# Compressed-key scores in a sparse-attention block: one matmul of 128 columns a head for two of 64, and a VectorE add for the second part

## The chip, the cores and the metric

The kernel runs on one core of a Trainium2 chip. The metric is the time of one execution in microseconds (us), the median of several runs; the profile comes from one further execution. In the profile, PE is TensorE's matrix multiply and PEld its load of weights, DVE is VectorE, ACT ScalarE, POOL GpSimd and SP SyncE.

## The reference

One decoder block on 1024 tokens of width 1024, in float32: a normalisation and an input projection, two branches side by side (sparse attention with 8 heads of 64 in 2 groups, and retention with 4 heads of 128), sigmoid gates that merge the branches, an output projection and a feed-forward network of width 2816. The sparse attention has three parts for each query: attention over compressed keys (one for each 16 tokens), over the 8 best blocks of 64 tokens, and over a window of 512. The change touches the first:

```python
kc = rms_norm(compress_blocks(k_cmp, cmp_pe[0], cmp_w1[0], cmp_w2[0]), k_g[0])
c_dist = (t_pos[:, None] - c_end[None, :]).astype(f32)
sc = jnp.einsum('btgrd,bngd->bgrtn', qg, kc).astype(f32) * scale - slopes[:, :, None, None] * c_dist
p_cmp = masked_softmax(sc, c_dist >= 0)
o_cmp = jnp.einsum('bgrtn,bngd->btgrd', p_cmp.astype(vc.dtype), vc)
...
imp = jnp.einsum('bgtn,nj->bgtj', p_cmp.sum(axis=2), overlap)
_, sel_idx = lax.top_k(imp, n_top)
```

So the weights over the compressed keys also choose which blocks the second part reads.

## The kernel before

Matmuls run on float32 values split in a high and a low part (`split`, L371: ScalarE copies the high part, VectorE subtracts it to get the low one), and a product is three matmuls, high by high, high by low and low by high. Every Python generator in the kernel (a stream) yields operations to a planner (`Sched`, L159). The planner keeps a clock of its own for each engine and a cost for each operation, and emits next the operation that it thinks can start first; equal ones go by priority. The instructions of an engine then stand in that order for good, with semaphores between the engines. Other costs in one place therefore change the order in many.

Attention works through 16 units `us` (2 groups of heads by 8 tiles of 128 queries). `cmp_all` (L1304) does the compressed part of a unit: the scores of the four heads of the group in one PSUM bank `s` (L1313 to L1315), then the scaled sum with the distance table Mc and the running minimum (`ttr`, L1299, a custom VectorE instruction that writes the probabilities' tile P and the minimum m; the profile has it as L1302 cP), the exponential on ScalarE, the reciprocal and the gate, and Pd, P doubled side by side and scaled, on POOL. Four transposes of Pd and a split make pcT, with which `consume_all` (L1440) starts the unit's output. From the fourth tile on `select` chooses the blocks and writes `comb`. `kc` holds the 64 compressed keys of a group twice: `kc[:, g, 0]` has high over low parts on its 128 partitions, `kc[:, g, 1]` the same with the parts exchanged; the stationary operand `qt[u][:, 0, r, :]` is the same for both, and L1314 and L1315 add the two products in PSUM.

`produce_all` (L1379) makes the scores of the window and of the chosen blocks (psS<-kT,qt, then L1302 P), and shares the two scores banks of `s_ring` (L1265) with `cmp_all`. `consume_all` transposes P (psT<-ident,P), splits it (pT) and multiplies with the values (psO<-pT,vv). `finish` sends a unit's output y to DRAM (`y_scr`).

What else is there runs between these as filler, with lower priority. `merge_gates` (L1270) makes the gates of the merge (psF or psS <-H,wh, then zs to `z_scr`). When the gates are done, `y_loads` brings the branches' outputs back from DRAM (yraw<-y_scr) and `y_split` writes them over H; `branch1` (L1559) multiplies the retention branch with its weights, sixteen outputs of twelve matmuls (psF<-H,wh), scales them with the gate (sg) and writes them to `u_scr`. `merge_main` (L1581) does the same for the attention branch: its first two outputs go to the banks of `f_ring` (psF), and behind them, in the order of the queue, the six banks S, S, S, O, T, T of `u_ring` (L1523) in turn, once the last unit's y is on its way (L1587). `mx_loads` (L1596) reads `u_scr` back into the mx tiles, which are allocated only when all of attention's memory is given back (L1626 to L1639), and `merge_out` (L1602) loads the gate (sgm<-z_scr), multiplies it with the output in PSUM, which frees the bank, and adds to mx. All these loads go through SyncE's one queue, in the planner's order. Behind the merge stand the output projection (psS<-wo,H) and the feed-forward network.

Of the kernel before, what the change touches and what calls it, by code (L numbers as in the profile page):

```python
# [9 lines left out]
F32 = mybir.dt.float32  # L10
# [3 lines left out]
ALU = mybir.AluOpType  # L14
# [26 lines left out]
def nel(ap):  # L41
    n = 1
    for d in ap.shape[1:]:
        n *= d
    return n
# [212 lines left out]
def kernel(  # L258
# [50 lines left out]
    def mm(o, l, r, start, stop):  # L309
        n = nel(r)  # L310
        c = max(108.0, n * RATE[0] + 3) if r.dtype == F32R else 4 * max(53.5, n * 0.4167 + 1)
        return Op("pe", c, 100, [o], [l, r],
                  lambda: pe.matmul(o, l, r, start=start, stop=stop, skip_group_check=True))  # L313

    def tr(o, i):
        if i.dtype == F32R:
            return Op("pe", 56, 100, [o], [i], lambda: pe.transpose(o.bitcast(F32R), i, identr))
        return Op("pe", 109, 100, [o], [i], lambda: pe.transpose(o, i, ident))  # L318

    def ac(o, i, scale=1.0, func=AF.Copy, bias=None, accum=None):  # L320
        kw, ins, outs, c = {}, [i], [o], (51 if i.tensor.name.startswith("ps") else 93) + 0.833 * nel(o)
        for a in (scale, bias, accum):
            if a is not None and not isinstance(a, float):
                c += 93
        if bias is not None:
            kw["bias"] = bias
            ins.append(bias)
        if accum is not None:
            kw["accum_out"] = accum
            outs.append(accum)  # L330
        if not isinstance(scale, float):
            ins.append(scale)
        return Op("act", c, 150, outs, ins, lambda: act.activation(o, i, func, scale=scale, **kw))  # L333

    def vop(o, ins, fn, eng=None, fast=False):
        n = nel(o)
        if eng is gp:
            return Op("gp", 70 + 2.4 * n, 150, [o], ins, fn)
        c = 61 if any(nel(i) == 1 < n for i in ins) else 0
        return Op("dve", 69 + c + (0.52 if fast else 1.04) * n, 130, [o], ins, fn)  # L340

    def tt(o, a, b, op, eng=None):
        return vop(o, [a, b], lambda: (eng or dve).tensor_tensor(o, a, b, op), eng)  # L343

    def ts(o, a, s1, s2=None, op0=ALU.mult, op1=None, eng=None, fast=True):
        ins = [a] + [s for s in (s1, s2) if s is not None and not isinstance(s, (int, float))]
        if op1 is None:
            return vop(o, ins, lambda: (eng or dve).tensor_scalar(o, a, s1, None, op0=op0), eng, fast)  # L348
        return vop(o, ins, lambda: (eng or dve).tensor_scalar(o, a, s1, s2, op0=op0, op1=op1), eng, fast)

    def stt(o, a, s, b, op0, op1, eng=None):
        ins = [a, b] + ([] if isinstance(s, float) else [s])
        return vop(o, ins, lambda: (eng or dve).scalar_tensor_tensor(o, a, s, b, op0=op0, op1=op1), eng)  # L353

    def recip(o, i):
        return vop(o, [i], lambda: dve.reciprocal(o, i))
# [118 lines left out]
    kc = att.tile([128, 2, 2, HD], F32R, name="kc")  # L475
# [4 lines left out]
    Mc = att.tile([128, 128], F32, name="Mc")[:, 0:120]  # L480
# [344 lines left out]
    qt, qref = {}, {}  # L825
# [12 lines left out]
    def q_drop(u):  # L838
        qref[u] -= 1
        if not qref[u]:  # L840
            rings["q"].release(qt[u])
# [392 lines left out]
    ap_ = es.enter_context(tc.tile_pool(name="ap", bufs=2))  # L1234
# [64 lines left out]
    def ttr(o, a, b, sc, init, acc):  # L1299
        ins = [a, b] + ([] if isinstance(init, float) else [init])  # L1300
        return Op("dve", (77 if isinstance(init, float) else 138) + 1.04 * nel(o), 130, [o, acc], ins,
                  lambda: dve.tensor_tensor_reduce(o, a, b, -sc, init, ALU.add, ALU.min, acc))  # L1302

    def cmp_all():  # L1304
        yield Wait(lambda: "ct" in fl)
        for u in us:
            g, i = u
            yield Wait(lambda: u in qt)
            P = ap_.tile([128, 4, 64], F32, name="cP", bufs=1)
            l = small.tile([128, 4], F32, name="cl")  # L1310
            m = small.tile([128, 4], F32, name="cm")
            s = yield Alloc(s_ring)
            for r in range(4):  # L1313
                yield mm(s[:, r * 64:(r + 1) * 64], qt[u][:, 0, r, :], kc[:, g, 0, :], True, False)  # L1314
                yield mm(s[:, r * 64:(r + 1) * 64], qt[u][:, 0, r, :], kc[:, g, 1, :], False, True)  # L1315
            q_drop(u)
            for r in range(4):
                yield ttr(P[:, r, :], s[:, r * 64:(r + 1) * 64], Mc[:, 56 - 8 * i:120 - 8 * i],
                          2.0 ** -(4 * g + r + 1), 3e38, m[:, r:r + 1])
            s_ring.release(s)  # L1320
            for r in range(4):
                yield ac(P[:, r, :], P[:, r, :], scale=-1.0, func=AF.Exp, bias=m[:, r:r + 1], accum=l[:, r:r + 1])
            rl = small.tile([128, 4], F32, name="crl")
            c = small.tile([128, 4], F32, name="cc")
            yield recip(rl, l)
            yield tt(c, rl, gate[:, i, 4 * g:4 * g + 4, 0], ALU.mult)
            if i == 0:
                yield ts(c, c, valid0)
            Pd = ap_.tile([128, 4, 2, 64], F32, name="cPd", bufs=1)
            yield tt(Pd, P[:, :, None, :].to_broadcast([128, 4, 2, 64]),  # L1330
                     c[:, :, None, None].to_broadcast([128, 4, 2, 64]), ALU.mult, gp)
            if i >= 4:
                pn = ap_.tile([128, 4, 64], F32, name="cpn", bufs=1)
                yield tt(pn, P, rl[:, :, None].to_broadcast([128, 4, 64]), ALU.mult)
                yield stt(pn, pn, TINY, pn, ALU.is_ge, ALU.mult)
                sch.spawn(select(u, pn), 2)
            pt = yield Alloc(pc_ring)
            p = yield Alloc(t_ring)
            for r in range(4):
                yield tr(p[:, r * 128:(r + 1) * 128], Pd[:, r].rearrange("p a n -> p (a n)"))  # L1340
            yield ac(pt, p)
            yield tt(pt[64:128, :], p[64:128, :], pt[64:128, :].bitcast(F32), ALU.subtract)
            t_ring.release(p)
            pcT[u] = pt
            if i >= 4:
                yield Wait(lambda: ("imp", u) in fl)

    def select(u, pn):
        g, i = u
        yield Wait(lambda: "lt" in fl and "st" in fl)  # L1350
        im = ap_.tile([128, 3, 64], F32, name="cim", bufs=1)
        yield tt(im[:, 0:2], pn[:, 0:2], pn[:, 2:4], ALU.add, gp)
        yield tt(im[:, 2], im[:, 0], im[:, 1], ALU.add, gp)
        fl.add(("imp", u))
        iv = im[:, 2].rearrange("p (j f) -> p j f", f=4)
        v = ap_.tile([128, 4, 16], F32, name="cv", bufs=1)
        yield tt(v[:, 0], iv[:, :, 0], iv[:, :, 1], ALU.add, gp)
        yield tt(v[:, 1], iv[:, :, 2], iv[:, :, 3], ALU.add, gp)
        yield tt(v[:, 2], v[:, 0], v[:, 1], ALU.add, gp)
        yield tt(v[:, 2, 1:], v[:, 2, 1:], iv[:, :15, 3], ALU.add, gp)  # L1360
        yield tt(v[:, 2], v[:, 2], Fb[:, i - 4], ALU.add, gp)
        vj = v[:, 2, :, None].to_broadcast([128, 16, 16])
        vk = v[:, 2, None, :].to_broadcast([128, 16, 16])
        gt = ap_.tile([128, 2, 16, 16], F32, name="cgt", bufs=1)
        yield tt(gt[:, 0], vk, vj, ALU.is_equal)
        yield tt(gt[:, 1], vk, vj, ALU.is_gt)
        yield tt(gt[:, 0], gt[:, 0], Ltri, ALU.mult, gp)
        yield tt(gt[:, 0], gt[:, 0], gt[:, 1], ALU.add, gp)
        rk = small.tile([128, 16], F32, name="crk")
        yield rsum(rk, gt[:, 0])  # L1370
        yield ts(rk, rk, 7.5, NEG, ALU.is_ge, ALU.mult)
        nb = 2 * (i + 1)
        cb = yield Alloc(cb_ring)
        yield tt(cb[:, :nb * 64].rearrange("p (j s) -> p j s", s=64),
                 Mt[:, 896 - 128 * i:1024].rearrange("p (j s) -> p j s", s=64),
                 rk[:, :nb, None].to_broadcast([128, nb, 64]), ALU.add, gp)
        comb[u] = cb
# [135 lines left out]
    sch.spawn(consume_all(), 1)  # L1513
    sch.spawn(produce_all(), 1)
    sch.spawn(cmp_all(), 2)
    sch.spawn(merge_gates(), 8)

# [807 lines left out]
```

## Time and profile before

| | us |
|---|---|
| median of three runs (lowest, highest) | 1595.7 (1595.24, 1597.64) |
| the profiled execution, by the same clock | 1598.91 |
| its span, first to last instruction | 1597.2 |
| first and last kc matmul in it (start) | 380.6, 721.1 |
| last matmul of attention (psO<-pT,vv) until the next | 808.65 |

A row of a timeline gives the start, the duration, the engine, line, operation and names (output, arrow, inputs), and how many instructions it merges. In brackets stands the idle time of the engine before it and what ended that. Matmuls overlap in the records, so the time that one takes in a row of them is read from start to start. A row of the groups gives the count, the busy time, the mean of one in ns and the idle time before them.

### The profile page before, as it was taken

The numbers are of one execution on the slowest core, as the hardware profiler recorded it, in microseconds if no ns is written. First come the engines' busy times: TensorE is split into PE (matmuls) and PEld (weight loads), VectorE is DVE, ScalarE is ACT, GpSimd is POOL, SyncE is SP. The second block draws the span as 40 slices with busy tenths as digits, with TensorE's granted clock in tenths as the row PEclk, the third lists the DMA queues.
The fourth block names the chain that finished last, engine by engine and source line by source line (L and its number), as shares of the span: only waits on it lengthen the run. The fifth ranks groups of instructions, "written<-read, shape, count | busy, mean of one in ns | idle before, by whom it ended". The sixth has DMA issues, their size and how long they took to land.

```text
span 1597.2 us, 23177 instructions
## 1 busy us (share of the span) xinstructions
PE 1558.2 (98%) x8299; PEld 1339.0 (84%) x8299; DVE 1034.4 (65%) x2163; ACT 742.4 (46%) x1512; POOL 294.2 (18%) x387
## 2 busy tenths in 40 slices
PE   8989999998999999999999999999999999999999
PEld 8989888887989898897887887888888888788887
DVE  7346655543798967789839449656666555477674
ACT  6234343333777667677524326333333333344442
POOL 4233100002132211221000101332343332000000
PEclk9999999999999999999999999999999999999999
DMA  5565364326333245225476322534344544397521
GB/s 179 159 170 159 111 183 119 118 86 192 99 100 119 81 139 165 73 78 179 140 257 211 132 80 80 184 132 142 135 134 150 178 141 141 120 403 256 180 78 53
DMA packets 191573, 233.06 MB, mean 146 GB/s; under 512 B 21857, under 2 KB 123233, under 8 KB 191202
## 3 DMA queue, kind: packets, MB, share of 16 engines
q1 hardware_dynamic: 178978, 193.84, 37.5%
q0 software_dynamic: 12480, 37.75, 7.1%
q8 instruction: 65, 1.06, 0.3%
q14 instruction: 50, 0.41, 0.1%
HBM read 159.18 MB, written 72.37 MB: 145 GB/s over the span
## 4 chain that ended last, share of the span: by engine, by line
PE 81%; DVE 5%; DMA 3%; ACT 1%; issue 1%; POOL 0%; SPq 0%; DVEq 0%; ACTq 0%
PE psS L313 27%; PE psF L313 26%; PE psO L313 12%; PE psT L313 11%; PE psT L318 4%; DMA qt<-q_scr 1%; DVE P L1302 1%; DMA mx<-u_scr 1%; DVE pT L343 1%; PE psF L318 0%; DVE H L343 0%; DVE wh L343 0%; DMA sg<-z_scr 0%; DVE P L348 0%; DVE T L343 0%
## 5 line engine op out<-in xcount | busy, mean ns | idle before, releaser
L313 PE MATMUL psF<-H,wh 128*128 128x512 f32 x780 | 200.2, 394 | 4.7 <-DVE H L343 2.8
L313 PE MATMUL psS<-H,wh 128*128 128x512 f32 x684 | 187.2, 404 | 3.9 <-DVE sgm L353 3.1
L313 PEld LDWEIGHTS psF<-H,wh 128*128 128x128 f32 x780 | 142.9, 188 | 31.0 <-DVE H L343 3.3
L313 PEld LDWEIGHTS psS<-H,wh 128*128 128x128 f32 x684 | 126.5, 192 | 25.7 <-issue 3.5
L333 ACT ACTIVATE P<-P,pm 128x640 f32<-128x640 f32 (+7 forms) x128 | 94.1, 735 | 45.8 <-DVE pm L1302 43.4
L343 DVE TENSOR_TENSOR pT<-psT,pT 128x512 fp32r<-128x512 f32 (+1 forms) x152 | 92.1, 615 | 32.9 <-ACT pT L333 32.6
L313 PE MATMUL psS<-kT,qt 128*128 128x384 f32 (+3 forms) x384 | 102.9, 346 | 1.0 <-ACT zs L333 0.9
L333 ACT ACTIVATE pT<-psT 128x512 fp32r<-128x512 f32 (+1 forms) x152 | 77.7, 533 | 42.9 <-PE psT L318 42.5
L313 PE MATMUL psO<-pT,vv 128*128 128x256 f32 x528 | 91.3, 290 | 1.8 <-DVE pT L343 1.7
L313 PE MATMUL psS<-whA,H 128*128 128x256 f32 (+1 forms) x672 | 89.9, 288 | 0.0
L313 PEld LDWEIGHTS psO<-pT,vv 128*128 128x128 f32 x528 | 79.2, 189 | 11.2 <-DVE pT L343 4.1
L313 PEld LDWEIGHTS psS<-whA,H 128*128 128x128 f32 x672 | 83.6, 189 | 0.0
L318 PE MATMUL psT<-ident,P 128*128 128x128 f32 x528 | 77.2, 273 | 0.2 <-DVE pT L343 0.2
L313 PEld LDWEIGHTS psS<-kT,qt 128*128 128x128 f32 x384 | 65.7, 192 | 8.1 <-ACT zs L333 1.1
L343 DVE TENSOR_TENSOR wh<-wraw,wh 128x512 fp32r<-128x512 f32 (+1 forms) x55 | 52.3, 959 | 23.1 <-ACT wh L333 23.0
L318 PEld LDWEIGHTS psT<-ident,P 128*128 128x128 f32 x528 | 61.2, 140 | 4.0 <-issue 0.6
L366 POOL DMA_DIRECT2D qt<-q_scr x16 | 12.4, 775 | 280.7 <-DMA r_scr<-gt 189.6
L333 ACT ACTIVATE op<-T 128x512 fp32r<-128x512 f32 x55 | 34.6, 630 | 61.6 <-PE psT L313 34.1
L333 ACT ACTIVATE wh<-wraw 128x512 fp32r<-128x512 f32 (+1 forms) x55 | 44.0, 810 | 32.2 <-PE psT L313 9.9
L343 DVE TENSOR_TENSOR op<-T,op 128x512 fp32r<-128x512 f32 x55 | 48.9, 893 | 15.3 <-ACT op L333 14.4
L313 PE MATMUL psS<-wo,H 128*128 128x512 f32 x216 | 58.6, 393 | 0.0
L313 PE MATMUL psS<-op 128*128 128x512 f32 x234 | 57.6, 389 | 0.0
(505 smaller groups left out, 3556.8 us busy)
## 6 DMA issues: line engine op xcount, KB each, us to landing
wraw<-in_w_in_dram SPq DMA_DIRECT2D x24, 512.0 KB, 4.5
row<-in_ffn_w_down_dram POOLq DMA_DIRECT2D x22, 512.0 KB, 6.0
f_scr<-fs SPq DMA_DIRECT2D x22, 512.0 KB, 2.6
t_scr<-row POOLq DMA_DIRECT2D x22, 512.0 KB, 3.1
qt<-q_scr POOLq DMA_DIRECT2D x16, 512.0 KB, 4.3
st<-t_scr SPq DMA_DIRECT2D x31, 256.0 KB, 5.1
z_scr<-zs SPq DMA_DIRECT2D x24, 256.0 KB, 2.1
wraw<-in_ffn_w_gate_dram SPq DMA_DIRECT2D x12, 512.0 KB, 3.7
```

The lines of the kernel that those rows point to most:

```text
L313: lambda: pe.matmul(o, l, r, start=start, stop=stop, skip_group_check=True))
L318: return Op("pe", 109, 100, [o], [i], lambda: pe.transpose(o, i, ident))
L333: return Op("act", c, 150, outs, ins, lambda: act.activation(o, i, func, scale=scale, **kw))
L343: return vop(o, [a, b], lambda: (eng or dve).tensor_tensor(o, a, b, op), eng)
L366: r = Op("gp", 1040, 0, [o], [i], lambda: gp.dma_start(o, i)) if eng is gp else \
L1302: lambda: dve.tensor_tensor_reduce(o, a, b, -sc, init, ALU.add, ALU.min, acc))
```

## The change

Per head there is one matmul with all 128 columns of `kc[:, g]`, both versions side by side, instead of two of 64 that add up in PSUM. A head's two partial scores then lie side by side in the bank, which is now full (4 x 128 columns, before 4 x 64). VectorE adds the second parts of all four heads to the table Mc in a new tile cS of 128 x 256, and the four `ttr` read cS where they read Mc.

```diff
             for r in range(4):
-                yield mm(s[:, r * 64:(r + 1) * 64], qt[u][:, 0, r, :], kc[:, g, 0, :], True, False)
-                yield mm(s[:, r * 64:(r + 1) * 64], qt[u][:, 0, r, :], kc[:, g, 1, :], False, True)
+                yield mm(s[:, r * 128:(r + 1) * 128], qt[u][:, 0, r, :], kc[:, g].rearrange("p a n -> p (a n)"), True, True)
             q_drop(u)
+            sv = s.rearrange("p (r a n) -> p r a n", r=4, a=2)
+            sm = ap_.tile([128, 4, 64], F32, name="cS", bufs=1)
+            yield tt(sm, sv[:, :, 1], Mc[:, None, 56 - 8 * i:120 - 8 * i].to_broadcast([128, 4, 64]), ALU.add)
             for r in range(4):
-                yield ttr(P[:, r, :], s[:, r * 64:(r + 1) * 64], Mc[:, 56 - 8 * i:120 - 8 * i],
+                yield ttr(P[:, r, :], sv[:, r, 0], sm[:, r],
                           2.0 ** -(4 * g + r + 1), 3e38, m[:, r:r + 1])
```

The planner costs the matmuls and the new add, so the order moves on every engine from the first unit on. Two places matter here. On TensorE, at the end of attention: psO<-pT,vv are the last products with the values, psT<-ident,P the transposes ahead of them, psF<-H,wh the end of `branch1` and the first two outputs of `merge_main`, and psS, psO and psT <-H,wh the six banks of `merge_main`. Before:

```order
L313 MATMUL psO<-pT,vv_6499 128x256 x4
L318 MATMUL psT<-ident,P 128x128 x4
L313 MATMUL psF<-H,wh 128x512 x6
L313 MATMUL psO<-pT,vv_6499 128x256 x4
L313 MATMUL psF<-H,wh 128x512 x3
L313 MATMUL psO<-pT,vv_6499 128x256 x4
L313 MATMUL psF<-H,wh 128x512 x52
L313 MATMUL psS<-H,wh 128x512 x36
L313 MATMUL psO<-H,wh 128x512 x12
L313 MATMUL psT<-H,wh 128x512 x24
```

The same place on TensorE in the changed kernel:

```order
L313 MATMUL psO<-pT,vv_6560 128x256 x4
L318 MATMUL psT<-ident,P 128x128 x4
L313 MATMUL psF<-H,wh 128x512 x4
L313 MATMUL psO<-pT,vv_6560 128x256 x8
L313 MATMUL psS<-H,wh 128x512 x36
L313 MATMUL psO<-H,wh 128x512 x12
L313 MATMUL psT<-H,wh 128x512 x24
```

The 52 psF matmuls that stood behind the last product of attention stand ahead of it now, spread over attention; the rows from psS on are the same.

On SyncE, just behind that, where `u_scr` is written and mx and the gates sgm are loaded. Before (the numbers in u_scr and z_scr tell the tiles of DRAM apart):

```order
L367 DMA yraw<-y_scr_133 64x512 x8
L367 DMA u_scr_132<-sg 128x512 x2
L367 DMA wraw<-in_w_branch_dram 128x4x256
L367 DMA g_9259<-in_norm_g_dram 128x1024
L367 DMA mx<-u_scr_125 128x512
L367 DMA sgm<-z_scr_0_7967 128x512
L367 DMA mx<-u_scr_126 128x512
L367 DMA sgm<-z_scr_0_7312 128x512
L367 DMA mx<-u_scr_125 128x512
L367 DMA mx<-u_scr_126 128x512
```

The same place on SyncE in the changed kernel:

```order
L367 DMA u_scr_132<-sg 128x512 x2
L367 DMA wraw<-in_w_branch_dram 128x4x256
L367 DMA y_scr_133<-y_9188 128x4x128
L367 DMA yraw<-y_scr_133 64x512 x8
L367 DMA g_9231<-in_norm_g_dram 128x1024
L367 DMA mx<-u_scr_125 128x512
L367 DMA sgm<-z_scr_0_7586 128x512
L367 DMA mx<-u_scr_126 128x512
L367 DMA sgm<-z_scr_0_6987 128x512
L367 DMA mx<-u_scr_125 128x512
L367 DMA sgm<-z_scr_0_7586 128x512
```

The last two writes of `u_scr` now stand ahead of the last y, and a third sgm load stands behind the third mx load, where it stood behind all sixteen.

## The prediction

> **What bounds the kernel now.** I read the page first, then the table by stretches, then TensorE's waits, and last the timelines around the end of attention.
>
> ```profile
> span 1597.2 us, 23177 instructions
> PE 1558.2 (98%) x8299; PEld 1339.0 (84%) x8299; DVE 1034.4 (65%) x2163; ACT 742.4 (46%) x1512; POOL 294.2 (18%) x387
> ```
>
> TensorE is busy for 98% of the span, so a matmul less can be worth its time, but only where TensorE has other work behind it. The stretches show where that holds (busy us of each engine, then granted clock, DMA share and GB/s; attention is the second and third stretch):
>
> ```profile
> core 0: us, PE busy (x) PEld busy (x) DVE busy (x) ACT busy (x) POOL busy (x), PEclk, DMA share, GB/s
> 380.00:740.00 360.00, 352.11 (x2294) 315.98 (x2294) 284.14 (x992) 260.52 (x659) 81.94 (x154) 0.99 0.36 113
> 740.00:808.65 68.65, 67.62 (x403) 59.67 (x404) 57.28 (x129) 40.21 (x71) 2.29 (x1) 1.00 0.54 172
> 808.65:840.05 31.40, 28.29 (x126) 23.12 (x125) 10.42 (x15) 5.04 (x6) 0.00 (x0) 1.00 0.89 304
> 840.05:1597.20 757.15, 747.93 (x3316) 617.68 (x3316) 485.39 (x689) 293.08 (x512) 138.86 (x138) 1.00 0.45 154
> ```
>
> In attention TensorE idles 7.9 + 1.0 = 8.9 us of 428.7, although VectorE (79% and 83%) sets much of the pace: the gate and branch products (H,wh) are filler that the planner puts wherever attention's own matmuls would wait. Attention ends at 808.65, and the stretch behind it is of another kind:
>
> ```profile
> 808.17 0.64 PE L313 MATMUL psO<-pT,vv 128*128 128x256 f32 x4
> 808.65 11.98 PE L313 MATMUL psF<-H,wh 128*128 128x512 f32 x52
> 820.46 8.32 PE L313 MATMUL psS<-H,wh 128*128 128x512 f32 x36
> 828.62 2.88 PE L313 MATMUL psO<-H,wh 128*128 128x512 f32 x12
> 831.34 5.60 PE L313 MATMUL psT<-H,wh 128*128 128x512 f32 x24
> 840.05 10.02 PE L313 MATMUL psS<-H,wh 128*128 128x512 f32 x36 [3.11 <-DVE sgm L353]
> ```
>
> Call 808.65 E. After it stand 52 filler matmuls (820.46 - 808.65 = 11.81 us, 0.227 each), then six output banks of the last branch, then a wait of 3.1 us. What that wait hangs on is a chain of transfers that runs meanwhile on SyncE's queue and VectorE:
>
> ```profile
> 809.47 0.37 SPq L367 DMA_DIRECT2D y_scr<-y  x1
> ...
> 811.64 4.95 SPq L367 DMA_DIRECT2D yraw<-y_scr  x8
> ...
> 822.28 0.33 SPq L367 DMA_DIRECT2D mx<-u_scr  x1
> ...
> 824.08 9.65 SPq L367 DMA_DIRECT2D mx<-u_scr  x14
> 834.04 1.68 SPq L367 DMA_DIRECT2D sgm<-z_scr  x3
> ```
> ```profile
> 820.83 0.69 DVE L343 TENSOR_TENSOR H<-yraw,H 128x512 fp32r<-128x512 f32 x1 [0.70 <-ACT H L333]
> ...
> 839.22 1.36 DVE L353 SCALAR_TENSOR_TENSOR sgm<-sgm,psS 128x512 f32<-128x512 f32 x2 [7.05 <-DMA sgm<-z_scr]
> ```
> ```profile
> 817.32 4.88 DMA u_scr<-sg
> ...
> 834.04 5.15 DMA sgm<-z_scr
> ```
>
> The last y goes out to DRAM and back, and its last split ends at 821.52 (E + 12.9). The mx tiles take memory of the tiles before them and start at 822.28 (E + 13.6), when the last u_scr write has landed (817.32 + 4.88). The third gate load (sgm) is issued behind all sixteen mx loads, at 834.04, and its landing (5.15 us later) lets VectorE empty the first of the six banks. So E to 840.05 is 31.4 us of latency, and the 52 + 72 matmuls only cover it.
>
> **The change, part by part.** First the matmuls themselves. In the timeline of a unit's scores, and of 128-column matmuls a little later:
>
> ```profile
> 391.20 1.06 PE L313 MATMUL psS<-kc,qt 128*128 128x64 f32 x8
> 392.09 0.66 PE L318 MATMUL psF<-ident,rt 128*128 128x128 f32 x4
> ```
> ```profile
> 407.03 0.39 PE L313 MATMUL psF<-rd,re 128*128 128x128 f32 x2
> 407.25 0.39 PE L313 MATMUL psF<-rS,rc 128*128 128x128 f32 x2
> ```
>
> Eight of 64 columns take 392.09 - 391.20 = 0.89 us from start to start, 0.111 each. Two of 128 columns take 407.25 - 407.03 = 0.22, 0.11 each: the width is free here, since every matmul brings a weight load of its own. So 4 instead of 8 saves 4 x 0.111 = 0.44 us a unit and 16 x 0.44 = 7.1 us in all. Bounds: nothing saved (if the column count set the price) and 7.1. I take 7.1, since the 128-column row is that of the new width. The page "TensorE: Matmul & The Clock Gate" of the Trainium skill, section "Back-to-back issue gap", speaks against it: it gives about 60 cycles to 1-64 columns and 134 to 128, by which four wide ones would cost slightly more than eight narrow ones. The trace disagrees, with 0.111 and 0.11 us; the rule is kept as the rival "nothing saved" below.
>
> Second, VectorE's add over 128 x 256, not in the trace. Nearest rows, a copy out of PSUM with a subtraction and the scaled product of the same chain:
>
> ```profile
> 748.23 0.42 DVE L343 TENSOR_TENSOR pT<-psT,pT 128x256 fp32r<-128x256 f32 x1
> 748.57 0.68 DVE L1302 CUSTOM_DVE_ANT_0 P<-psS,comb 128x512 f32<-128x512 f32 x1
> ```
> ```profile
> L348 DVE TENSOR_SCALAR P<-P,pc 128x640 f32<-128x640 f32 (+7 forms) x61 | 33.6, 569 | 1.2
> ...
> L353 DVE SCALAR_TENSOR_TENSOR sg<-sg,psF 128x512 f32<-128x512 f32 x13 | 8.8, 678 | 0.4 <-PE psF L313 0.4
> ```
>
> It lasts 0.42 and the next starts after 0.34, so 16 adds cost 5.4 us of VectorE (6.7 at most, if nothing overlaps). The four reductions a unit keep their shape and form; their second operand is now a fresh tile, but in the same memory and written by the same engine, so nothing is added there. The planner moves work as well: before the last split of attention, the order counts 61 scalings of P on VectorE before and 53 after (8 x 0.57 = 4.6 us, which go to ScalarE, 72% busy in the second stretch), and 13 branch products sg before and 16 after (3 x 0.68 = 2.0 us). VectorE's net is 5.4 - 4.6 + 2.0 = +2.8 us until E. What is queued behind the add is the same unit's four reductions, and for them wait ScalarE's exponentials; the scores' bank is held 0.34 longer by the add and 0.44 less by the matmuls, so the second scores bank comes free as before.
>
> Third, the order on TensorE, which decides. The 52 filler matmuls that stood behind E now stand all in front of it (the two pieces of TensorE's order above); from the first kc matmul to E nothing else is added or lost. So TensorE's work up to E changes by +52 x 0.227 - 7.1 = 11.8 - 7.1 = +4.7 us. With waits as before, E moves from 808.65 to 813.35. A split of attention that gets shorter on TensorE and still takes more filler means that the planner found attention's own chain longer.
>
> Fourth, the stretch behind E. Its cover of 11.8 us is gone and TensorE goes at once to the six banks. Of the first unit there, the parts of the last y need the split at E + 12.9 (chain as in the rows above: its transfers do not depend on the filler). About 9 of the 72 matmuls can run before, 63 x 0.227 = 14.3 us behind: the six banks are done at E + 27.2. The mx loads no longer wait for u_scr, which is written before E; they start at E + 13.0, with the split. SyncE's order has the third sgm load ahead of thirteen mx loads now, so it lands by about 13.0 + 2.2 + 5.15 = E + 20.4 (five issues ahead of it at 0.45, from 824.08 - 822.28 = 1.8 for four), and the first bank is free before TensorE wants it: twelve matmuls (2.7 us) run to E + 29.9. The next bank hangs on the fourth sgm, behind all mx loads as the third was before: 13.0 + (834.04 - 822.28) + 0.4 for the inserted issue + 5.15 to land + 0.69 on VectorE + 0.15 from there to TensorE = E + 31.2. Before, that bank's matmuls began 2.7 after 840.05, at E + 34.1. So 2.9 us come back. From there on TensorE's order is the same, and it is packed (9.2 us idle in 757).
>
> Sum: +4.7 - 2.9 = **+1.8 us**. The profiled execution took 1598.91 by the device's clock (span 1597.2); the median of the three timed runs is 1595.7, and I add to that: **1597.5 us**. A measurement here can tell about 0.2% (3.2 us) from no change, so this counts as the same.
>
> **The rivals.** (A) *Slower: VectorE, not TensorE, sets E.* The adds come on top of TensorE's longer queue, because the in-order TensorE then waits at QK products whose bank VectorE has not emptied. Its price is between the net 2.8 and the full 5.4: E + 7.5 to 10.1, in all +4.6 to +7.2, say 1601.7. For it: VectorE at 83% before E. Against: TensorE's waits on VectorE are small,
>
> ```profile
> PE psF L313 <- DVE H L343: 2.8, 1, 2.8
> PE psO L313 <- DVE pT L343: 1.7, 3, 0.7
> ...
> PE psS L313 <- DMA qt<-q_scr: 0.3, 1, 0.3
> ```
>
> of which the 2.8 is the change from gates to branch products. (The last row is why I cost nothing for the q loads that change places with comb and cPd on POOL's queue: in attention TensorE waits 0.3 us for them; a load that came late would hold all of TensorE's queue behind its scores.) It decides as soon as VectorE's own waits for TensorE are used up. (B) *Faster: the filler that moved in falls into idle time.* TensorE has 8.9 us of it before E; half of it covered brings the time to 1597.5 - 4.5 = 1593, all of it to 1588.6, say 1591. Against: these are many waits of under 1 us in an in-order queue. (C) *The early sgm load gains nothing*, because the mx loads still start late or the load lands late: +4.7, 1600.4. (D) *Nothing saved*: the wide matmuls cost double, +7.1: 1604.6.
>
> **How the numbers follow.** Forecast 0.50, A 0.25, B 0.15, C 0.05, D 0.05. The forecast's own scatter is 1593.5 to 1600, since the planner's new order changes dozens of small waits: of its 0.50 I give 0.03 to faster, 0.36 to same, 0.11 to slower. B gives 0.105 faster and 0.045 same; A 0.21 slower, 0.04 same; C and D 0.095 slower and 0.005 same. That makes faster 0.135, same 0.45, slower 0.415. The range 1591 to 1603.5 leaves out the lower half of B, D and the top of A.
>
> **What would show it.** Right: kc rows of 128 columns at 0.11 from start to start; adds of about 0.42; E near 813; TensorE idle for some 10 us just behind E and again until about E + 31; the rest as long as before. Wrong: E at or before 809 (B), E past 816 with TensorE waiting for VectorE's reductions (A), the six banks' next matmuls at E + 34 (C), kc at 0.2 (D).

## The result, and the profile after

| | median us (lowest, highest) | runs | ratio to the kernel before, 95% interval |
|---|---|---|---|
| before, on the same chip | 1596.67 (1595.24, 1597.95) | 4 | |
| changed | 1617.91 (1616.8, 1620.32) | 4 | 1.0135 [1.0118, 1.0153] |

The changed kernel is slower by 21 us, 1.35%. That is outside the range. The page of the changed kernel:

```profile
span 1618.5 us, 23056 instructions
PE 1559.8 (96%) x8235; PEld 1335.3 (83%) x8235; DVE 1035.4 (64%) x2174; ACT 746.8 (46%) x1517; POOL 294.4 (18%) x387
```

TensorE runs 64 instructions less, and the span is 21.3 us longer. No engine got more work worth speaking of, so the time is waiting, or the same work done more slowly. The same stretches as before show where (the bounds are moved to the new E and to the start of the next bank that waits):

```profile
core 0: us, PE busy (x) PEld busy (x) DVE busy (x) ACT busy (x) POOL busy (x), PEclk, DMA share, GB/s
380.00:740.00 360.00, 343.23 (x2156) 306.21 (x2157) 277.58 (x958) 251.75 (x633) 78.73 (x144) 0.97 0.39 118
740.00:828.14 88.14, 86.79 (x529) 76.93 (x529) 70.62 (x177) 54.70 (x103) 8.89 (x13) 1.00 0.42 135
828.14:858.88 30.74, 22.05 (x87) 16.84 (x85) 8.49 (x13) 3.98 (x5) 0.00 (x0) 0.83 0.75 264
858.88:1618.50 759.62, 746.83 (x3304) 614.87 (x3304) 482.12 (x688) 293.14 (x512) 136.51 (x137) 1.00 0.45 153
```

E, the end of attention, went from 808.65 to 828.14: +19.5, where +4.7 was forecast. In attention TensorE idles 16.8 + 1.35 = 18.1 us (before 8.9) and is busy 10.3 us more (430.0 for 419.7), of which the order explains 4.7. The other 5.6 fall together with a lower granted clock, 0.97 for 0.99 in the first stretch. So 19.5 = 4.7 of work + 9.2 of idle + 5.6 of slow work. The stretch behind E came out as forecast:

```profile
827.04 1.26 PE L313 MATMUL psO<-pT,vv 128*128 128x256 f32 x8
828.14 1.56 PE L313 MATMUL psS<-H,wh 128*128 128x512 f32 x6
837.33 1.65 PE L313 MATMUL psS<-H,wh 128*128 128x512 f32 x3 [7.63 <-ACT H L333]
839.83 7.96 PE L313 MATMUL psS<-H,wh 128*128 128x512 f32 x27 [0.85 <-ACT H L333]
...
858.88 5.84 PE L313 MATMUL psS<-H,wh 128*128 128x512 f32 x24 [0.20 <-DVE sgm L353]
...
880.54 9.84 PE L313 MATMUL psS<-wo,H 128*128 128x512 f32 x35 [2.01 <-DVE sgm L353]
```

TensorE waits 7.63 + 0.85 us for the last y to come back. The bank for which E + 31.2 was forecast starts at 858.88, E + 30.7 (before E + 34.1). But the 3.4 us do not last: at 880.54 the output projection waits for VectorE, which is still emptying the merge's banks, and behind that pause 48 of its matmuls take 12.6 us, where 49 took 11.1 before (the granted clock is 0.58 from 880 to 884). From E to the end of the span it is 790.4 us now and was 788.6.

The attention stretch is where VectorE's in-order queue stands still. Its waits there, in us, times, longest; before, the only wait for a transfer at ry was 0.5 us long:

```profile
DVE ry L353 <- DMA y_scr<-ry: 7.5, 2, 4.7
DVE ry L353 <- DMA rb<-r_scr: 5.8, 1, 5.8
```

ry is the last step of the retention branch, another stream than the one that was changed (L1203 to L1206): two halves of 512 tokens go one after the other through one buffer ry, each multiplied with a gate from rb and written to `y_scr`. VectorE's timeline, where it is worst:

```profile
606.54 1.35 DVE L343 TENSOR_TENSOR pT<-psT,pT 128x512 fp32r<-128x512 f32 x2
613.69 0.75 DVE L353 SCALAR_TENSOR_TENSOR ry<-psF,few,rb 128x512 f32<-128x512 f32 x1 [5.79 <-DMA rb<-r_scr]
619.15 0.75 DVE L353 SCALAR_TENSOR_TENSOR ry<-psF,few,rb 128x512 f32<-128x512 f32 x1 [4.71 <-DMA y_scr<-ry]
619.81 0.28 DVE L1302 CUSTOM_DVE_ANT_0 P<-psS,Mw 128x128 f32<-128x128 f32 x1
```

The two halves stand next to each other in the queue. The second may not overwrite ry before the first has been written out, and everything behind it on VectorE, the scores of attention first (P<-psS), stands still too: 10.5 us of two waits, with one instruction of 0.75 us between them. The chain of waits shows the two transfers (start, duration):

```profile
606.28 7.32 DMA rb<-r_scr
...
614.47 4.55 DMA y_scr<-ry
```

In the kernel before, the same load was issued at 600.54 and its half of ry ran at 606.72, so it had landed. TensorE's side of it:

```profile
614.50 1.42 PE L313 MATMUL psF<-H,wh 128*128 128x512 f32 x5 [1.04 <-DVE ry L353]
...
620.16 0.44 PE L313 MATMUL psS<-kT,qt 128*128 128x128 f32 x2 [2.42 <-DVE pm L1302]
```

TensorE itself waits only 3.5 us there, since it has filler. The units' outputs y come 4.2 us later than before at the fourth unit, 10.2 at the fifth, 14 to 15 at the seventh and eighth, and 23.3 at the ninth, the first one behind these rows. So most of the delay is older than these rows, and most of the step at the ninth unit is work: between the eighth y and the ninth, TensorE runs 61 filler matmuls (H,wh) where it ran 27, and 34 x 0.227 = 7.7 us of the 9.0. These rows show the mechanism at its longest, not where most of the loss was made.

The one buffer holds VectorE in two earlier heads too, with no load beside it. In the first head TensorE waits just behind it:

```profile
437.75 0.75 DVE L353 SCALAR_TENSOR_TENSOR ry<-psF,few,rb 128x512 f32<-128x512 f32 x1 [2.83 <-DMA y_scr<-ry]
```
```profile
439.15 0.62 PE L313 MATMUL psO<-pT,vv 128*128 128x256 f32 x3 [2.12 <-DVE pT L343]
```

In the third head VectorE stands 2.85 us before the second half (557.00). The waits by releaser put that down to TensorE (psS), but the chain of waits runs through the write of ry:

```profile
552.91 3.96 DMA y_scr<-ry
```

### The profile page after: what moved, and what is told of

It reads as the page before. It is cut to its first block, busy times and chain, and to the rows that moved or that the text cites. A ratio compares the mean times of both kernels' runs of the same rounds, so it can differ in the third digit from the quotient of the medians.

```text
span 1618.5 us, 23056 instructions
## 1 busy us (share of the span) xinstructions
PE 1559.8 (96%) x8235; PEld 1335.3 (83%) x8235; DVE 1035.4 (64%) x2174; ACT 746.8 (46%) x1517; POOL 294.4 (18%) x387
## 4 chain that ended last, share of the span: by engine, by line
PE 77%; DVE 6%; DMA 4%; ACT 2%; issue 2%; POOL 0%; SPq 0%; DVEq 0%; ACTq 0%; POOLq 0%
PE psF L313 26%; PE psS L313 24%; PE psO L313 11%; PE psT L313 11%; PE psT L318 4%; DVE P L1302 1%; DMA y_scr<-ry 1%; DMA sgm<-z_scr 1%; DVE pT L343 1%; DMA yraw<-y_scr 1%; DVE H L343 0%; ACT P L333 0%; DMA rb<-r_scr 0%; SPq L367 0%; DMA st<-in_ffn_w_down_dram 0%
## 5 line engine op out<-in xcount | busy, mean ns | idle before, releaser
L313 PE MATMUL psF<-H,wh 128*128 128x512 f32 x780 | 206.1, 398 | 7.8 <-DVE H L343 4.9
L333 ACT ACTIVATE op<-T 128x512 fp32r<-128x512 f32 x55 | 34.6, 630 | 61.5 <-PE psT L313 34.1
L333 ACT ACTIVATE P<-P,pc 128x640 f32<-128x640 f32 (+7 forms) x75 | 50.4, 698 | 15.7 <-DVE pc L343 15.5
```

## The experiments

Theory O says that the time comes from the new order that the planner writes down, not from the instructions that were changed, and within it from the waits for the one buffer ry. The rivals are the add on VectorE (the prediction's A), the filler moved ahead of E, and an order that was lucky before or unlucky after. Runs whose base isn't named are edits of the changed kernel.

**1. The new instructions in the order of before.** The planner is shown the old operations, and the new ones are emitted in their places.

```diff
                 yield mm(s[:, r * 128:(r + 1) * 128], qt[u][:, 0, r, :], kc[:, g].rearrange("p a n -> p (a n)"), True, True)
+                yield Op("pe", 108.0, 100, [s], [qt[u], kc], lambda: None)
...
-            yield tt(sm, sv[:, :, 1], Mc[:, None, 56 - 8 * i:120 - 8 * i].to_broadcast([128, 4, 64]), ALU.add)
...
+                o = ttr(P[:, r, :], sv[:, r, 0], sm[:, r], 2.0 ** -(4 * g + r + 1), 3e38, m[:, r:r + 1])
+                o.ins = [key(s), key(Mc)]
+                if r == 0:
+                    def both(f=o.fn, sm=sm, sv=sv, mc=mc):
+                        dve.tensor_tensor(sm, sv[:, :, 1], mc[:, None, :].to_broadcast([128, 4, 64]), ALU.add)
+                        f()
+                    o.fn = both
+                yield o
```

The empty operation stands in the plan for the second matmul, and the first `ttr` of a unit issues the add ahead of itself.

> The changed instructions (four matmuls of 128 columns, the add, the reductions from the new tile) in the order that every engine had before: the planner is shown the old operations and costs. Theory O (the loss comes from the new order, not from the new instructions): 1588 to 1598 us, since TensorE has 7.1 us less and VectorE 5.4 us more in otherwise unchanged queues. Theory C (the added VectorE step lengthens attention wherever it stands): 1605 to 1618 us.

Measured: 1592.1 us, ratio 0.9969 [0.9955, 0.9983]: the change is worth 5 us when the order stays. The timeline at E:

```profile
801.94 0.64 PE L313 MATMUL psO<-pT,vv 128*128 128x256 f32 x4
802.42 11.98 PE L313 MATMUL psF<-H,wh 128*128 128x512 f32 x52
...
833.53 10.02 PE L313 MATMUL psS<-H,wh 128*128 128x512 f32 x36 [2.81 <-DVE sgm L353]
```

E is at 802.42, with the 52 filler matmuls behind it. The instructions are not the cause.

**2. The old instructions in the new order**, the mirror image: the planner sees the new costs, the old matmuls and the old `ttr` are emitted, and there is no add.

```diff
-                yield mm(s[:, r * 128:(r + 1) * 128], qt[u][:, 0, r, :], kc[:, g].rearrange("p a n -> p (a n)"), True, True)
+                o = mm(s[:, r * 64:(r + 1) * 64], qt[u][:, 0, r, :], kc[:, g, 0, :], True, False)
+                p = mm(s[:, r * 64:(r + 1) * 64], qt[u][:, 0, r, :], kc[:, g, 1, :], False, True)
+                def both(f=o.fn, h=p.fn):
+                    f()
+                    h()
+                o.fn = both
+                yield o
...
+            yield Op("dve", 69 + 1.04 * 256, 130, [sm], [s, Mc], lambda: None)
```

> The instructions of before (eight matmuls of 64 columns, no add) in the order that every engine has after the change: the planner is shown the new operations and costs. Theory O: 1613 to 1626 us, slow although nothing was added. Theory C: 1593 to 1603 us.

Measured: 1615.08 us, ratio 1.0117 [1.0102, 1.0133]. VectorE waits at ry as in the changed kernel:

```profile
DVE ry L353 <- DMA rb<-r_scr: 7.2, 1, 7.2
...
DVE ry L353 <- DMA y_scr<-ry: 4.4, 2, 2.6
DVE ry L353 <- PE psS L313: 3.0, 1, 3.0
```

Runs 1 and 2 together: the order costs 1.2% on the old instructions (1.0117) and 1.7% on the new ones (1.0135 over 0.9969).

**3. The changed kernel with a second buffer for ry**, in the memory of a tile that is dead by then. The order is the changed kernel's on every engine.

```diff
-                y32 = rp.tile([128, 512], F32, name="ry", bufs=1)
+                y32 = rp.tile([128, 512], F32, name="ry", tag="re" if half else "ry", bufs=1)
```

> The changed kernel, its order unchanged, but the retention output ry of the second half of a head lies in other memory (that of the product tile re, idle then), so that VectorE needs not wait until the first half has been written to DRAM. Theory O in the form that VectorE's waits at ry (17 us in the profile after, 7.5 of them for this write) carry the loss: 1606 to 1614 us. If those waits lie beside others: 1616 to 1619 us.

Measured: 1607.96 us, ratio 1.0073 [1.0054, 1.0092]. The two halves of the last head now run as one pair, with the wait for the load left:

```profile
603.32 1.41 DVE L353 SCALAR_TENSOR_TENSOR ry<-psF,few,rb 128x512 f32<-128x512 f32 x2 [5.94 <-DMA rb<-r_scr]
```
```profile
817.49 1.27 PE L313 MATMUL psO<-pT,vv 128*128 128x256 f32 x8
818.59 1.55 PE L313 MATMUL psS<-H,wh 128*128 128x512 f32 x6
```

By the ratios the single buffer carries 10 of the 21 us. In the traces E comes 9.6 earlier than in the changed kernel. Of these, 2.4 lie ahead of the first kc matmul, where ry has no part, and 7.2 in attention. They do not lie where the wait was longest: the third unit's y gains 3.1 us (behind the first head's ry) and the seventh's 3.8 (behind the third head's), while the ninth's loses 1.9 again. There, with VectorE's wait for the write gone, TensorE stands at the next load, for which it had waited 0.2 us in the changed kernel:

```profile
619.69 1.11 PE L313 MATMUL psS<-kc,qt 128*128 128x128 f32 x4 [3.88 <-DMA qt<-q_scr]
```

E is still 9.9 later than before.

**4. Run 3 with the wait for the load taken away too:** the first half of the gate is loaded early into a tile of its own.

```diff
+                if half:
+                    g0 = rp.tile([128, 512], F32, name="rt")
+                    def load2(f=q.fn, g0=g0, h=h):
+                        f()
+                        sp.dma_start(g0, r_scr[h][3][:, 0:512])
...
+            q.fn = lambda sgl=sgl, h=h: sp.dma_start(sgl[:, 512:1024], r_scr[h][3][:, 512:1024])
...
+                q = stt(y32, o, gng[:, h:h + 1], sgl[:, s] if half else g0, ALU.mult, ALU.mult)
```

> As the run with two buffers for ry, and the first half of retention's gate (sgl, the rb load of a head's end) is loaded together with the last q load, into memory that is idle then (rt); the second half stays where it was in SyncE's queue. All other queues stand as after the change. Theory O in the form that VectorE's in-order waits for transfers at ry carry the loss before the end of attention: another 2 to 6 us off, 1602 to 1606 us. If the wait for rb lies beside other waits: 1606.5 to 1609 us.

Measured: 1608.47 us, ratio 1.0062 [1.0043, 1.008], nothing that can be told from run 3. The wait for rb is gone, and others took its place on VectorE:

```profile
DVE yraw L343 <- DMA yraw<-y_scr: 12.9, 3, 8.2
...
DVE ry L353 <- PE psS L313: 4.7, 1, 4.7
```

In run 3 these were 9.0 for yraw and none for psS (the longest yraw wait, 8.2, lies behind E in both). The ninth to the thirteenth y come 2.8 us earlier than in run 3, and the fourteenth 0.8 later, behind a new wait of 4.2 us for yraw. A wait that has another just behind it is worth nothing by itself.

**5. Two ry buffers in the order of before** (run 1 as the base).

```diff
-                y32 = rp.tile([128, 512], F32, name="ry", bufs=1)
+                y32 = rp.tile([128, 512], F32, name="ry", tag="re" if half else "ry", bufs=1)
```

> The changed instructions in the order of before, with two buffers for ry as well. In that order VectorE waited at ry for 1.0 us in all, so if the ry buffer matters only where the order puts both halves together: 1591 to 1593 us, as without it. If it gains by itself, whatever the order: 1582 to 1588 us.

Measured: 1594.79 us, ratio 0.9981 [0.997, 0.9991]. No gain over run 1, whose VectorE waited 1.0 us for ry: the second buffer has a value only in an order that puts the halves together.

**6. The add done twice, in the order of before** (run 1 as the base).

```diff
                         dve.tensor_tensor(sm, sv[:, :, 1], mc[:, None, :].to_broadcast([128, 4, 64]), ALU.add)
+                        dve.tensor_tensor(sm, sv[:, :, 1], mc[:, None, :].to_broadcast([128, 4, 64]), ALU.add)
                         f()
```

> The changed instructions in the order of before, and each of the 16 adds issued twice in a row (the second writes the same values). If the add stands on the path of attention: plus 16 x 0.34 = 5.4 us on the run without it, 1596.5 to 1599 us. If the filler on TensorE covers it: 1591 to 1594 us.

Measured: 1600.7 us, ratio 1.0016 [1.0007, 1.0025]. The second add costs 5.9 us against run 5, on the same chip (where the second ry buffer changed nothing clear), and 0.0047 x 1597 = 7.5 by the ratios against run 1. The groups give the add's own size, here in the kernel of run 3:

```profile
L343 DVE TENSOR_TENSOR cS<-psS,Mc 128x256 f32<-128x256 f32 x16 | 6.7, 420 | 20.7 <-PE psS L313 20.6
```

16 x 0.42 = 6.7 us: the second add is paid in full.

**7. No add, in the order of before** (run 1 as the base; the second part of the scores is left out).

```diff
-                        dve.tensor_tensor(sm, sv[:, :, 1], mc[:, None, :].to_broadcast([128, 4, 64]), ALU.add)
...
-                o = ttr(P[:, r, :], sv[:, r, 0], sm[:, r], 2.0 ** -(4 * g + r + 1), 3e38, m[:, r:r + 1])
+                o = ttr(P[:, r, :], sv[:, r, 0], mc, 2.0 ** -(4 * g + r + 1), 3e38, m[:, r:r + 1])
```

> The matmul part alone, in the order of before: four matmuls of 128 columns, and no add; the reductions read the first part of the scores and the table Mc, so the second part of the scores is left out of the result. If TensorE's 7.1 us come through whole: 1588 to 1590.5 us. If the add costs its 5.4 us, this lies 4 to 6 us under the run with the add (1586 to 1588); if it costs nothing, at 1591 to 1593.

Measured: 1591.59 us, ratio 0.996 [0.9946, 0.9974]. Against before that is -6.4 us (7.1 were reckoned for the matmuls), and it is 1.4 us below run 1 by the ratios, whose intervals overlap, and 3.2 below run 5 on the same chip. The first add is hidden for half or more of its 6.7 us, the second is not.

**8. The kernel before, with the 64 reductions planned 10 ns dearer.** No instruction is changed, only the order.

```diff
+                o = ttr(P[:, r, :], s[:, r * 64:(r + 1) * 64], Mc[:, 56 - 8 * i:120 - 8 * i],
+                        2.0 ** -(4 * g + r + 1), 3e38, m[:, r:r + 1])
+                o.cost += 10.0
+                yield o
```

> The kernel before, with one number changed that only the planner sees: 10 ns more for each of the 64 reductions over compressed keys. No instruction changes, the order does. If any shift of the order costs about as much as this change did (the order of before is a lucky one): 1604 to 1622 us. If the loss belongs to this change's own order: 1593 to 1600 us.

Measured: 1610.01 us, ratio 1.0086 [1.0065, 1.0107], with 27 filler matmuls behind E. A nudge of 0.64 us in the plan costs 14 us on the chip.

**9. The same with 2 ns.**

```diff
-                o.cost += 10.0
+                o.cost += 2.0
```

> The kernel before with its old instructions; the planner reckons each of the 64 reductions of the compressed scores 2 ns dearer, nothing else. Its list keeps the two halves of the retention output ry apart (5 to 11 instructions of VectorE between them, as before) and leaves 32 psF matmuls behind the end of attention, E, where before left 52. Theory O (what costs is the waits of VectorE that an order brings, not the amount of filler ahead of E): the ry waits stay small, and the time moves only by the filler, 20 x 0.227 = 4.5 us at E and less at the end: 1596 to 1602. Rival L (the order of before was a lucky one and any other costs ten or more, as a nudge of 10 ns did): 1606 to 1612, E at 815 or later.

Measured: 1600.02 us, ratio 1.0008 [0.9994, 1.0022]. Theory O's range holds, and rival L falls: the order of before is not the only good one. At E:

```profile
810.62 0.63 PE L313 MATMUL psO<-pT,vv 128*128 128x256 f32 x4
811.09 7.43 PE L313 MATMUL psF<-H,wh 128*128 128x512 f32 x32
...
842.51 5.76 PE L313 MATMUL psS<-H,wh 128*128 128x512 f32 x24 [0.92 <-DVE sgm L353]
```

20 filler matmuls less stand behind E (32 for 52), and the next bank starts at E + 31.4. This is the prediction's sum in small, 20 x 0.227 = 4.5 at E and 2.7 back behind it, and the time agrees within its interval: in this order, where VectorE waits 1.8 us for ry, moving 20 filler matmuls costs next to nothing.

**10. The nudge of 10 ns with two ry buffers** (run 8 as the base).

```diff
-                y32 = rp.tile([128, 512], F32, name="ry", bufs=1)
+                y32 = rp.tile([128, 512], F32, name="ry", tag="re" if half else "ry", bufs=1)
```

> The kernel before nudged by 10 ns a reduction (1610.0 us), with the second half of the retention output ry in memory of its own, same order on every engine. Its VectorE waited 2.6 us for the writes of ry. Theory O: those waits go, and with them 3 to 6 us: 1604 to 1607. Rival L (dozens of small waits make the difference, none of which matters by itself): 1608 to 1611.

Measured: 1615.13 us (1607.03 to 1616.94), ratio 1.009 [1.0063, 1.0118], its median above both ranges. Theory O misses here: the waits for the writes of ry, 2.6 us in run 8, are gone, and no time with them. A candidate in its place is the load of another tile of retention, for which TensorE waits in the same part of attention, first in run 8, then here:

```profile
609.22 2.08 PE L313 MATMUL psF<-rc,rb 128*128 128x128 f32 x8 [4.27 <-DMA rc<-r_scr]
```
```profile
613.47 1.16 PE L313 MATMUL psF<-rc,rb 128*128 128x128 f32 x8 [3.90 <-DMA rc<-r_scr]
```

Whether that load carries the 14 us was not tried.

**11. Run 3 with the filler held back:** the stream of the merge's gates is ranked 500 ns later, and 97 filler matmuls stand behind E.

```diff
-    sch.spawn(merge_gates(), 8)
+    sch.spawn(merge_gates(), 8, 500.0)
```

> The changed kernel with two ry buffers (1608.0 us), and the stream that feeds the gate products of the merge to the planner ranked 500 ns later, so that attention's own work goes first: 97 psF matmuls now stand behind E, where the changed kernel had none and before had 52. Rival F (filler ahead of E holds up attention's chain, so taking it away gives more than its own time back): E near 818 - 97 x 0.227 = 796 or earlier, and as the 97 and the 72 matmuls behind E then cover the loads there up to E + 38, the end comes about 10 to 15 us earlier: 1593 to 1598. Theory O (VectorE's waits hold attention, whatever TensorE does meanwhile): E at 806 to 812, the end no earlier than with the filler ahead: 1604 to 1609.

Measured: 1603.71 us, ratio 1.0042 [1.0028, 1.0057], 5 us better than run 3 by the ratios, between the two ranges. E:

```profile
800.12 0.63 PE L313 MATMUL psO<-pT,vv 128*128 128x256 f32 x4
800.59 11.28 PE L313 MATMUL psF<-H,wh 128*128 128x512 f32 x49
815.06 13.96 PE L313 MATMUL psF<-H,wh 128*128 128x512 f32 x48 [3.19 <-DVE sg L353]
...
847.41 10.04 PE L313 MATMUL psS<-H,wh 128*128 128x512 f32 x36 [2.07 <-DVE sgm L353]
```

E is 18.0 earlier than in run 3, less than the time of the 97 matmuls themselves (22.0). So nothing here shows that filler ahead of E holds up attention beyond its own time. Nor is ry what holds it up by now: in this run VectorE waits for no transfer there, and attention, its filler taken off, is no shorter than in run 3. Behind E, 97 are more than the loads need as cover: from E to the end of the span it is 806.3 us, for 788.0 in run 3. The traced execution (1608.97 us) was the longest of the five, so the gain of the median does not show in it.

**12. The changed kernel with the add planned 60 ns dearer**, another order of the same instructions.

```diff
+            o = tt(sm, sv[:, :, 1], Mc[:, None, 56 - 8 * i:120 - 8 * i].to_broadcast([128, 4, 64]), ALU.add)
+            o.cost += 60.0
```

> The changed kernel, whose planner reckons the new add 60 ns dearer: another order of the same instructions, with no filler behind E either. The last two halves of ry stand back to back on VectorE again, with one buffer. Theory O (the orders that keep the one-buffer ry together and all filler ahead of E cost this): 1610 to 1619, with VectorE waiting 4 us or more for writes of ry and loads ahead of it. Rival L' (the order of the changed kernel was an unlucky draw among its own): 1598 to 1606.

Measured: 1614.07 us, ratio 1.0104 [1.0084, 1.0124]. Theory O's range holds. The last two halves of ry stand together again, and VectorE waits as was expected:

```profile
DVE ry L353 <- DMA y_scr<-ry: 5.0, 2, 3.8
...
DVE ry L353 <- PE psS L313: 2.7, 1, 2.7
```

## Why the prediction was wrong

The step that failed is the third: "With waits as before, E moves from 808.65 to 813.35." The order was read for which matmuls stand on which side of E, and its waits were taken over from a trace of another order. They did not carry over: E moved 14.8 us further. Runs 1 and 2 show that the order does this with either set of instructions. Run 3 shows that 7.2 us of it, as the traces have it, are one buffer, and that most of it was lost at the first and the third head. The planner costs a `y_scr` write at its issue alone and does not know that ry is reused, so nothing keeps the two halves apart: in the order of VectorE of before, the second half came 6 to 10 rows behind the first; now it is 2, 6 and 3 rows, and in the last head they are neighbours.

Point by point:

- **The matmuls, right.** Four of 128 columns take 0.48 us from start to start (the rows below), 0.12 each, where 0.11 was taken. Run 7 gives 6.4 us for 7.1. Rival D, the double price, is refuted.

```profile
390.47 0.64 PE L313 MATMUL psS<-kc,qt 128*128 128x128 f32 x4
390.95 0.62 PE L318 MATMUL psF<-ident,rt 128*128 128x128 f32 x4
```

- **The add, right in size and too dear in the sum.** It takes 0.42 as the upper bound had it. In the order of before it costs 1.4 to 3.2 us, since attention waits for it only in part. Only a second one is paid in full (run 6).
- **Rival A, its sign right and its mechanism wrong.** E did go past 816, with TensorE waiting longer for VectorE's reductions (psS <- pm, 2.9 us for 0.5). But A put it down to the adds, and with the adds in the order of before the kernel is faster than before (run 1). A's price of 4.6 to 7.2 us is near that of a second add (5.9 to 7.5).
- **Rival B, refuted.** TensorE's idle time in attention doubled (18.1 us for 8.9), with all the filler in it.
- **The filler, right as far as it went.** Its move is +11.8 at E by its own time. Run 9 has a part of it, and there the sum holds within the interval.
- **The stretch behind E, right in place and too good in what it left.** The chain came at E + 30.7 for E + 31.2, but the words "From there on TensorE's order is the same, and it is packed" missed that the bank gained only brings forward the next wait, 2.01 us for the merge's VectorE work at 880.54. Rival C is refuted as it was put (its sign was E + 34), though its sum, nothing gained, is what came out.

The size of it all, by spans, over the 21.3 us: the first kc matmul starts 0.4 later and E - kc grows by 19.1, of which 4.7 are work; run 3 shortens E - kc by 7.2, to 439.9 from 447.1 with the start 2.4 earlier in that run. Behind E it is +1.8. Against run 1, which has the same instructions, E - kc is 22.9 longer: 11.8 by the moved filler, which is not given back behind E (790.4 us for 788.9), 7.2 by the one buffer, and 4.0 by neither. What stays open is this rest, which run 3 has too: its E is 16.2 later than that of run 1 with the same instructions, 11.8 by filler and 4.4 by waits and a slower clock that were not separated. Open too is what makes the order of run 8 slow. The order of before was a good one, though not the only one: of four other orders with one buffer (the changed kernel's, runs 8, 9 and 12) only run 9's is as fast, and the rest cost 0.9 to 1.35%.

The version that beats both kernels is run 1, the new instructions in the old order: 1592.1 us.

## What to carry to other kernels

Where a planner sets a fixed order, a change has two prices, that of its instructions and that of the order it brings, and they can be measured apart by emitting the new instructions in the old order and the old ones in the new. Before carrying waits over from an old trace, look in the new order at every single-buffered tile that a transfer empties: if two writers of it now stand closer together than the transfer takes, the whole in-order queue behind the second one waits. Its price is not its length: here the longest of these waits had another load just behind it, and taking it away gained nothing there. Such a buffer's reuse belongs into the planner's model, or the tile gets a second buffer.

## What the runs showed of the hardware

Pauses of TensorE can cost more than their length. The changed kernel in stretches of 4 us, behind the pauses of 2.12 us (until 439.15) and 1.44 us (until 559.28), which follow the waits for ry in the first and the third head, and of 2.42 us (until 620.16) and 4.92 us (until 726.21). The third figure from the end is the granted clock, 0.50 to 0.69 behind each of them:

```profile
440.00:444.00 4.00, 4.00 (x17) 3.48 (x16) 1.43 (x8) 2.23 (x10) 0.00 (x0) 0.57 0.90 264
...
560.00:564.00 4.00, 4.00 (x19) 3.76 (x20) 2.45 (x14) 2.64 (x9) 0.00 (x0) 0.60 0.44 152
...
618.00:622.00 4.00, 1.84 (x10) 1.67 (x11) 2.01 (x12) 1.44 (x7) 0.00 (x0) 0.90 0.33 127
622.00:626.00 4.00, 4.00 (x19) 3.57 (x18) 2.90 (x15) 3.28 (x14) 0.40 (x1) 0.67 0.70 220
...
724.00:728.00 4.00, 1.79 (x4) 1.50 (x5) 4.00 (x8) 1.25 (x3) 1.01 (x1) 0.50 0.43 109
728.00:732.00 4.00, 4.00 (x20) 3.53 (x19) 3.96 (x12) 1.73 (x4) 0.00 (x0) 0.69 0.92 267
```

The length alone does not decide. The changed kernel kept its clock behind a pause of 1.47 us (until 393.05), and the kernel before had one of 2.82 us (until 735.95) at the place of the 4.92, and kept it too:

```profile
732.00:736.00 4.00, 1.18 (x6) 0.62 (x4) 4.00 (x8) 3.73 (x7) 1.92 (x2) 1.00 0.65 181
736.00:740.00 4.00, 3.39 (x15) 2.40 (x15) 4.00 (x8) 1.76 (x4) 0.00 (x0) 1.00 0.78 231
```

In run 3 these pauses of the first and the third head are gone, and the clock reads 1.00 in both places, so a part of what the second buffer gains is clock. All this fits the 5.6 us by which TensorE was busy longer than its work explains; it was not tried by itself. The page "TensorE: Matmul & The Clock Gate" of the Trainium skill, section "Part 1: The HAM clock gate (the "warmup" mystery)", has half the clock after an idle window of about 3.4 us and as long a window until it is back. The pause of 4.92 us agrees with it, and the clock is back at 1.00 within 5 us of its end (from 731); the other three were shorter, 1.44 to 2.42 us, and lost the clock all the same.
